# Starting layer 0 on half a tile and one weight chunk, with the rotary angles on GpSimd

## The chip, the cores and the metric

One core of one Trainium2 chip runs the whole kernel. The metric is device time in microseconds (us), the median of three runs. Engines are named as in the profile: PE is TensorE (matmuls), DVE VectorE, ACT ScalarE, POOL GpSimd, SP the engine that issues the DMAs here.

## The reference, cut to what matters

Two layers of a streaming encoder on a sequence of 256 rows and 1024 columns, in float32. Each layer is a hybrid mixer, a cross-attention and a SwiGLU block, each with a residual and a layer norm. Only the start of the first mixer is touched:

```
def rope(x, pos):
    half = x.shape[-1] // 2
    inv_freq = ROPE_BASE ** (-jnp.arange(half, dtype=jnp.float32) / half)
    ang = pos.astype(jnp.float32)[..., None] * inv_freq
    ...
    cos, sin = jnp.cos(ang), jnp.sin(ang)
...
def hybrid_mixer(x, pos, w_in, ...):
    h = x @ w_in
    a_qkv, b_cq, b_ckv, b_kr, c_qkv, c_f, g = split_cols(h, ...)
    y_a = chunked_relpos_attention(a_qkv[:, :, 0], a_qkv[:, :, 1], a_qkv[:, :, 2], a_rel_bias)
    y_b = mla_attention(b_cq, b_ckv, b_kr, pos, b_q_norm, b_kv_norm, b_w_uq, b_w_ukv)
```

The kernel begins with the 384 columns `b_cq` (PSUM tile `l0c`, one for each half of the rows), goes on with `b_ckv`, `b_kr`, `c_f` (PSUM tile `l0r`, 296 columns) and then the columns of `a_qkv` (PSUM tile `l0a`). `cos` and `sin` (tables `cc` and `ss`) rotate `b_kr` and, later, the queries of the second mixer.

## The kernel before

The rows of x are two tiles of 128 (t = 0, 1). A matmul contracts over partitions, so x is transposed on PE in eight blocks of 128 columns for each tile, four to a PSUM tile `x_t`. ACT then copies that PSUM tile to `xTh`, rounded to the matmul format, and DVE subtracts to get the rest, `xTl`. Weights come from DRAM in chunks (`raw`) and are split the same way: ACT writes `hi` (line 90), DVE writes `lo` (line 91). Each product is three matmuls, hi x hi, lo x hi and hi x lo. `raw` has three buffers, so chunk n+3 is loaded when chunk n is split.

`Chunks` keeps this stream going. `load_first` issues the first loads, `next` hands out a chunk and splits ahead. Chunks 0 and 1 are the upper and lower 512 rows of the weights for `b_cq`. Each is split in four pieces, one block of 128 rows each. Chunks 2 and 3 belong to `l0r`, chunks 4 to 7 to the four `l0a` tiles.

The order of instructions on each engine is fixed when the program is built: a scheduler walks the code, and `tc.issue_after` and priorities set what may come ahead of what. Engines then run their own lists in order and wait for each other through semaphores. Before the first real matmul PE runs `warm_up`, matmuls of the identity that nobody reads: five at the very start and six after the transposes of tile 0.

`queries(t)` does chunk 0 and then chunk 1 for tile t into `l0c`; `late=True` puts the four products with `xTl` last in each chunk. `finish(1)`, the transposes of tile 1, follows `queries(0)`. `keys(t)` makes `l0r`. The matmul results live in a pool of four PSUM banks: `l0c` and `l0r` take all four, and the four `l0a` tiles that follow need a bank that has been read out. `rotary_tables` is made once, on DVE and ACT, after the splits for the first four chunks are placed; the rows at lines 610 to 614, which read `l0r`, need its result.

Of the kernel before, what the change touches and what calls it, by code (L numbers as in the profile page):

```python
# [24 lines left out]
QL = 384  # L25
KVL = 256
NOPE = 64
ROPE = 32
# [4 lines left out]
MAGIC = 12582912.0  # L33
NEG = -1.0e30
PRIO = 400
# [13 lines left out]
class Chunks:  # L49
# [25 lines left out]
    def _split(self, i):  # L75
        kts, cols, _, slots, heads = self.plan[i]
        raw = self.raw.pop(i)
        pool, tags = (self.split_pool, ("hi", "lo")) if slots is None else (self.slot_pool, slots)
        hi = pool.tile([P, kts, cols], F32R, tag=tags[0], name=f"hi{i}")
        lo = pool.tile([P, kts, cols], F32R, tag=tags[1], name=f"lo{i}")  # L80
        n = 4 if i < 2 else 2
        for h in range(n):
            c = (slice(None), slice(None), slice(h * cols // 2, (h + 1) * cols // 2))
            if kts % 2 == 0:
                c = (slice(None), slice(h * kts // n, (h + 1) * kts // n))
            a, b, r = hi[c], lo[c], raw[c]
            if heads:
                r = r.rearrange("p k (h e d) -> p k e h d", h=heads, e=2)
                a, b = (z.rearrange("p k (e h d) -> p k e h d", h=heads, e=2) for z in (a, b))
            self.nc.scalar.copy(a, r)  # L90
            self.last_split = self.nc.vector.tensor_tensor(  # L91
                out=b, in0=r, in1=a.bitcast(F32), op=ALU.subtract
            )
        self.parts[i] = (hi, lo)
# [33 lines left out]
def encoder_kernel(  # L128
# [32 lines left out]
    W = Chunks(nc, rawp, splitp, big, 5, 1)  # L161
    for l in range(L):
# [3 lines left out]
        for c in range(2):  # L166
            r = slice(512 * c, 512 * (c + 1))
# [50 lines left out]
        xt = resid.tile([P, D], F32, tag=f"x{t}", name=f"x{t}")  # L218
        x.append(xt)

    def x_load(t):
        for h in range(2):
            c = slice(512 * h, 512 * (h + 1))
            nc.sync.dma_start(x[t][:, c], x_in[0, t * P : (t + 1) * P, c])


    x_load(0)
    W.load_first(2)
    x_load(1)
    W.load_first(4)  # L230
    ident = const.tile([P, P], F32, tag="ident", name="ident")
    make_identity(nc, ident)
# [8 lines left out]
    def load(dst, src):  # L241
        with tc.issue_after(W.last.ins):
            nc.sync.dma_start(dst, src)
# [16 lines left out]
    cc = const.tile([P, 2, ROPE], F32, tag="cc", name="cc")  # L260
    ss = const.tile([P, 2, ROPE], F32, tag="ss", name="ss")

    def rotary_tables():
        half = ROPE // 2
        pos_i = const.tile([P, 2], I32, tag="pos_i", name="pos_i")
        load(pos_i, positions)
        pos = const.tile([P, 2], F32, tag="pos", name="pos")
        nc.vector.tensor_copy(pos, pos_i)
        freq = const.tile([P, half], F32, tag="freq", name="freq")
        for i in range(half):  # L270
            nc.gpsimd.memset(freq[:, i : i + 1], 10000.0 ** (-i / half))
        halfpi = const.tile([P, 1], F32, tag="halfpi", name="halfpi")
        nc.gpsimd.memset(halfpi, math.pi / 2)
        ang = const.tile([P, 2, half], F32, tag="ang", name="ang")
        for t in range(2):
            nc.vector.tensor_scalar(
                out=ang[:, t], in0=freq, scalar1=pos[:, t : t + 1], scalar2=None, op0=ALU.mult
            )
        n = const.tile([P, 2, half], F32, tag="turn", name="turn")
        nh = const.tile([P, 2, half], F32, tag="turn_h", name="turn_h")  # L280
        nc.vector.tensor_scalar(
            out=n, in0=ang, scalar1=1.0 / (2 * math.pi), scalar2=MAGIC, op0=ALU.mult, op1=ALU.add
        )
        nc.vector.tensor_scalar(out=n, in0=n, scalar1=MAGIC, scalar2=None, op0=ALU.subtract)
        nc.vector.tensor_scalar(
            out=nh, in0=n, scalar1=1.0 / 4096, scalar2=MAGIC, op0=ALU.mult, op1=ALU.add
        )
        nc.vector.tensor_scalar(
            out=nh, in0=nh, scalar1=MAGIC, scalar2=4096.0, op0=ALU.subtract, op1=ALU.mult
        )  # L290
        nc.vector.tensor_tensor(out=n, in0=n, in1=nh, op=ALU.subtract)
        c1 = 6.28125
        c2 = round((2 * math.pi - c1) * 2**20) / 2**20
        c3 = 2 * math.pi - c1 - c2
        for c in (c1, c2, c3):
            for part in (nh, n):
                nc.vector.scalar_tensor_tensor(
                    out=ang, in0=part, scalar=-c, in1=ang, op0=ALU.mult, op1=ALU.add
                )
        lim = 3.1415925  # L300
        nc.vector.tensor_scalar(
            out=ang, in0=ang, scalar1=lim, scalar2=-lim, op0=ALU.min, op1=ALU.max
        )
        nc.scalar.activation(ss[:, :, half:], ang, AF.Sin)
        nc.vector.scalar_tensor_tensor(
            out=n, in0=ang, scalar=-1.0, in1=ang, op0=ALU.mult, op1=ALU.max
        )
        nc.scalar.activation(cc[:, :, 0:half], n, AF.Sin, bias=halfpi, scale=-1.0)
        nc.vector.tensor_copy(cc[:, :, half:], cc[:, :, 0:half])
        nc.vector.tensor_scalar(  # L310
            out=ss[:, :, 0:half], in0=ss[:, :, half:], scalar1=-1.0, scalar2=None, op0=ALU.mult
        )


    kpe = const.tile([P, 2, P], F32, tag="kpe", name="kpe")
# [13 lines left out]
            nc.vector.tensor_tensor(out=lo, in0=ps, in1=hi.bitcast(F32), op=ALU.subtract),  # L329
        )  # L330

    def transpose_in(src, hi, lo, t, name, prio=2 * PRIO):

        for g in range(2):
            ps = abank(f"{name}_t{t}{g}")
            for k in range(4):
                nc.tensor.transpose(
                    ps[:, k * P : (k + 1) * P], src[:, (4 * g + k) * P : (4 * g + k + 1) * P], ident
                )
            with tc.high_priority(prio):  # L340
                ins = split_out(
                    hi[:, 4 * g : 4 * g + 4, t * P : (t + 1) * P],
                    lo[:, 4 * g : 4 * g + 4, t * P : (t + 1) * P],
                    ps.rearrange("p (k q) -> p k q", k=4),
                )
        return ins
# [13 lines left out]
    def as_(ps, w, c, k0, act, t, kts, start=True, stop=True, at=None, late=False):  # L360

        hi, lo = w
        ah, al = act
        s = slice(t * P, (t + 1) * P)
        last = None

        def low(k):
            nonlocal last
            last = mm(ps, al[:, k0 + k, s], hi[:, k, c], start=False, stop=stop and k == kts - 1)  # L369

        for k in range(kts):
# [147 lines left out]
    def mixer(l, finish):  # L519
# [8 lines left out]

        with ExitStack() as order:
            if l == 0:  # L530
                for ins in finish(0):
                    order.enter_context(tc.issue_after(ins.ins))
                warm_up(6)
                W.ahead_split = 0
                ww = [W.next() for _ in range(2)]
                W.ahead_split = 1
            else:
                ww = [W.next() for _ in range(4)]
        pc, pr = [], []

        def queries(t):
            ps = bank(f"{name}c{t}")
            as_(ps[:, 0:QL], ww[0], slice(0, QL), 0, xT, t, 4, True, False, late=True)
            pc.append(ps)
            return as_(ps[:, 0:QL], ww[1], slice(0, QL), 4, xT, t, 4, False, True, late=True)

        def keys(t):
# [6 lines left out]
        if l == 0:  # L554
            with tc.issue_after(queries(0).ins):
                second = finish(1)
            with ExitStack() as order:
                for ins in second:
                    order.enter_context(tc.issue_after(ins.ins))
                ww += [W.next() for _ in range(2)]  # L560
            queries(1)
            keys(0)
            keys(1)
        else:
            for t in range(2):
                queries(t)
                keys(t)
                if t == 0:
                    finish(1)

        if l == 0:
            with tc.issue_after(W.last_split.ins):
                rotary_tables()

        rel = bigtile(1, name + "rel")
        nc.gpsimd.memset(rel[0:64, :, 0:64], NEG)
# [16 lines left out]
        for t in range(2):  # L593
# [7 lines left out]
            for i, ps, a, n in parts:  # L601
# [12 lines left out]
            nc.vector.tensor_tensor(  # L614
                out=z[:, t], in0=pr[t][:, KVL + ROPE : KVL + ROPE + H], in1=bf, op=ALU.add
            )

        nc.vector.scalar_tensor_tensor(out=e, in0=z, scalar=-1.0, in1=z, op0=ALU.mult, op1=ALU.min)
        nc.scalar.activation(e, e, AF.Exp)
# [501 lines left out]
        gb = load_gains(4, ln_ffn_g[l], ln_ffn_b[l], name)  # L1121
        return out_proj(FT // 2, act, 2, gb, name, last=l == L - 1, tail=3, inside=True)

    finish = lambda t: transpose_in(x[t], xTh, xTl, t, "x0", 0)
    for l in range(L):
        finish = mixer(l, finish)
        finish = cross(l, finish)
# [33 lines left out]
```

## Time and profile before

| | us |
|---|---|
| median of three runs | 1026.73 |
| lowest, highest | 1026.42, 1027.92 |
| the profiled execution, its own time | 1027.47 |
| span of that execution in the profile | 1025.8 |
| PE busy in the span | 1013.6 |
| DVE, ACT, POOL busy | 686.3, 512.5, 117.0 |

The own time of the profiled execution holds 1.67 us that lie outside the span, and it is 0.74 us above the median. A time read in the trace counts from the start of the span.

### The profile page before, as it was taken

To read this page: it belongs to the slowest core of one execution; us is meant where nothing else is said; L and a number is where in the kernel's file an instruction comes from. 1 tells how busy PE (TensorE), PEld (TensorE's weight loads), DVE (VectorE), ACT (ScalarE), POOL (GpSimd) and SP (SyncE) were. 2 spreads that over 40 slices of the span, in tenths; PEclk is the share of its full clock that TensorE was granted. 3 is DMA by queue.
4 is the path that set the end of the run, shared out by engine and by line. 5 is a ranking of instruction groups with operands and counts; after the bars stand their busy time and mean duration, and the time that the engine had idled before them with its cause. 6 is when DMAs were issued, how large, how long until landed. Compare 5 with 4: busy or idle time off the path is not lost.

```text
span 1025.8 us, 18091 instructions
## 1 busy us (share of the span) xinstructions
PE 1013.6 (99%) x7494; PEld 954.0 (93%) x7494; DVE 686.3 (67%) x1164; ACT 512.5 (50%) x842; POOL 117.0 (11%) x156
## 2 busy tenths in 40 slices
PE   9999999999999999999999999999999999999997
PEld 8988999999998999998899889999989899999996
DVE  4879777757778555554776877767659785555445
ACT  5767555555455444443355775455444634444430
POOL 3100112512001000000021002052210010000001
PEclk9999999999999999999999999999999999999999
DMA  8755645466563656565556473534775454555631
GB/s 285 210 173 158 202 143 182 136 233 213 197 214 127 202 166 203 167 243 187 185 178 193 129 241 124 163 126 127 286 244 188 149 185 157 188 187 183 236 134 42
DMA packets 133651, 186.76 MB, mean 182 GB/s; under 512 B 6064, under 2 KB 108480, under 8 KB 132800
## 3 DMA queue, kind: packets, MB, share of 16 engines
q1 hardware_dynamic: 133568, 185.60, 54.7%
q8 instruction: 59, 0.97, 0.4%
q14 instruction: 24, 0.20, 0.1%
HBM read 182.42 MB, written 3.16 MB: 181 GB/s over the span
## 4 chain that ended last, share of the span: by engine, by line
PE 94%; DVE 2%; DMA 1%; POOL 1%; issue 0%; ACT 0%; SPq 0%; POOLq 0%; DVEq 0%
PE l0g L354 2%; PE l1g L354 2%; PE l1g L356 2%; PE l0g L356 2%; PE l1g L355 2%; PE l0g L355 2%; PE f1o L373 2%; PE f1o L372 2%; PE f1o L369 2%; PE f0o L373 2%; PE f0o L372 2%; PE f0o L369 2%; PE f0u L355 2%; PE f1u L354 2%; PE f0g L355 2%; PE f1g L355 2%
## 5 line engine op out<-in xcount | busy, mean ns | idle before, releaser
L91 DVE TENSOR_TENSOR lo<-raw,hi 128x1024 fp32r<-128x1024 f32 (+3 forms) x332 | 393.2, 1203 | 196.5 <-ACT hi L90 195.9
L90 ACT CAST hi<-raw 128x1024 fp32r<-128x1024 f32 (+3 forms) x332 | 330.1, 1017 | 312.4 <-issue 156.9
L354 PE MATMUL l0g<-xTh,hi 128*128 128x256 f32 x192 | 54.2, 282 | 0.0
L354 PE MATMUL l1g<-xTh,hi 128*128 128x256 f32 x192 | 54.2, 282 | 0.0
L356 PE MATMUL l1g<-xTh,lo 128*128 128x256 f32 x192 | 53.9, 281 | 0.0
L356 PE MATMUL l0g<-xTh,lo 128*128 128x256 f32 x192 | 53.9, 281 | 0.0
L355 PE MATMUL l1g<-xTl,hi 128*128 128x256 f32 x192 | 53.9, 281 | 0.0
L355 PE MATMUL l0g<-xTl,hi 128*128 128x256 f32 x192 | 53.9, 281 | 0.0
L385 POOL TENSOR_SCALAR f_r<-f_mv 128x1 f32<-128x1 f32 x4 | 3.3, 826 | 355.1 <-DVE f_mv L415 355.1
L373 PE MATMUL f1o<-lo,f1hh 128*128 128x256 f32 (+1 forms) x132 | 42.2, 320 | 0.0
L372 PE MATMUL f1o<-hi,f1hh 128*128 128x256 f32 (+1 forms) x132 | 42.1, 319 | 0.0
L369 PE MATMUL f1o<-hi,f1hl 128*128 128x256 f32 (+1 forms) x132 | 42.0, 318 | 0.0
L354 PE MATMUL f1g<-xTh,hi 128*128 128x256 f32 x144 | 40.5, 282 | 0.0
L354 PE MATMUL f0g<-xTh,hi 128*128 128x256 f32 x144 | 40.5, 282 | 0.0
L355 PE MATMUL f1g<-xTl,hi 128*128 128x256 f32 x144 | 40.5, 281 | 0.0
L355 PE MATMUL f0g<-xTl,hi 128*128 128x256 f32 x144 | 40.5, 281 | 0.0
L356 PE MATMUL f0g<-xTh,lo 128*128 128x256 f32 x144 | 40.5, 281 | 0.0
L356 PE MATMUL f1g<-xTh,lo 128*128 128x256 f32 x144 | 40.5, 281 | 0.0
L355 PE MATMUL f0u<-xTl,hi 128*128 128x256 f32 x144 | 40.5, 281 | 0.0
L356 PE MATMUL f0u<-xTh,lo 128*128 128x256 f32 x144 | 40.5, 281 | 0.0
L354 PE MATMUL f1u<-xTh,hi 128*128 128x256 f32 x144 | 40.5, 281 | 0.0
L354 PE MATMUL f0u<-xTh,hi 128*128 128x256 f32 x144 | 40.5, 281 | 0.0
(649 smaller groups left out, 3309.3 us busy)
## 6 DMA issues: line engine op xcount, KB each, us to landing
raw<-in_w_in SPq DMA_DIRECT2D x48, 1024.0 KB, 5.3
raw<-in_ffn_w_gu SPq DMA_DIRECT2D x44, 1024.0 KB, 5.1
raw<-in_ffn_w_down SPq DMA_DIRECT2D x22, 1024.0 KB, 4.8
raw<-in_w_branch SPq DMA_DIRECT2D x12, 1024.0 KB, 5.0
raw<-in_w_mix_out SPq DMA_DIRECT2D x8, 1024.0 KB, 4.8
raw<-in_xa_w_kv SPq DMA_DIRECT2D x8, 1024.0 KB, 5.0
raw<-in_xa_w_q SPq DMA_DIRECT2D x4, 1024.0 KB, 5.0
raw<-in_xa_w_o SPq DMA_DIRECT2D x4, 1024.0 KB, 4.9
```

What stands on the lines that cost most here:

```text
L90: self.nc.scalar.copy(a, r)
L91: self.last_split = self.nc.vector.tensor_tensor(out=b, in0=r, in1=a.bitcast(F32), op=ALU.subtract)
L354: mm(ps, hi[:, k, c], ah[:, k0 + k, :], start=start and k == 0, stop=False)
L355: mm(ps, hi[:, k, c], al[:, k0 + k, :], start=False, stop=False)
L356: mm(ps, lo[:, k, c], ah[:, k0 + k, :], start=False, stop=stop and k == kts - 1)
L369: last = mm(ps, al[:, k0 + k, s], hi[:, k, c], start=False, stop=stop and k == kts - 1)
L372: mm(ps, ah[:, k0 + k, s], hi[:, k, c], start=start and k == 0, stop=False)
L373: mm(ps, ah[:, k0 + k, s], lo[:, k, c], start=False, stop=False)
L385: nc.gpsimd.tensor_scalar(out=dst, in0=src, scalar1=scale, scalar2=eps, op0=ALU.mult, op1=ALU.add)
```

## The change

Five things are done to the first microseconds of layer 0.

- The second half of x's first tile is loaded after weight chunk 0 instead of before it, and `positions` is loaded second instead of after the chunks.
- Only the first half of tile 0 is transposed and only chunk 0 is split before the matmuls begin. The other half and chunk 1 come after the matmuls of chunk 0.
- The angles for the rotary tables are computed on GpSimd. The fused multiply-add of VectorE (`scalar_tensor_tensor`) becomes two GpSimd instructions, six times over.
- The absolute value stays on VectorE, the two sines on ScalarE; they are placed after the splits of chunks 0 to 3. The copy and the sign change that fill the tables go to GpSimd.
- What follows up to the exponential of the forget gate is placed after those splits too (`order`).

```diff
-    def x_load(t):
-        for h in range(2):
-            c = slice(512 * h, 512 * (h + 1))
-            nc.sync.dma_start(x[t][:, c], x_in[0, t * P : (t + 1) * P, c])
-    x_load(0)
+    def x_load(t, h):
+        c = slice(512 * h, 512 * (h + 1))
+        nc.sync.dma_start(x[t][:, c], x_in[0, t * P : (t + 1) * P, c])
+    pos_i = const.tile([P, 2], I32, tag="pos_i", name="pos_i")
+    x_load(0, 0)
+    nc.sync.dma_start(pos_i, positions)
+    W.load_first(1)
+    x_load(0, 1)
     W.load_first(2)
-    x_load(1)
+    x_load(1, 0)
+    x_load(1, 1)
     W.load_first(4)
...
-            nc.vector.tensor_scalar(
+            nc.gpsimd.tensor_scalar(
                 out=ang[:, t], in0=freq, scalar1=pos[:, t : t + 1], scalar2=None, op0=ALU.mult
             )
...
         for c in (c1, c2, c3):
             for part in (nh, n):
-                nc.vector.scalar_tensor_tensor(
-                    out=ang, in0=part, scalar=-c, in1=ang, op0=ALU.mult, op1=ALU.add
-                )
+                nc.gpsimd.tensor_scalar(out=pc, in0=part, scalar1=-c, scalar2=None, op0=ALU.mult)
+                nc.gpsimd.tensor_tensor(out=ang, in0=ang, in1=pc, op=ALU.add)
...
+    def rotary_tables():
+        ang, n, halfpi = angles
         nc.vector.scalar_tensor_tensor(
             out=n, in0=ang, scalar=-1.0, in1=ang, op0=ALU.mult, op1=ALU.max
         )
+        nc.scalar.activation(ss[:, :, half:], ang, AF.Sin)
         nc.scalar.activation(cc[:, :, 0:half], n, AF.Sin, bias=halfpi, scale=-1.0)
-        nc.vector.tensor_copy(cc[:, :, half:], cc[:, :, 0:half])
-        nc.vector.tensor_scalar(
+        nc.gpsimd.tensor_copy(cc[:, :, half:], cc[:, :, 0:half])
+        nc.gpsimd.tensor_scalar(
             out=ss[:, :, 0:half], in0=ss[:, :, half:], scalar1=-1.0, scalar2=None, op0=ALU.mult
         )
+    angles = rotary_angles()
...
             if l == 0:
-                for ins in finish(0):
+                for ins in finish(0, (0,)):
                     order.enter_context(tc.issue_after(ins.ins))
                 warm_up(6)
                 W.ahead_split = 0
-                ww = [W.next() for _ in range(2)]
-                W.ahead_split = 1
+                ww = [W.next()]
...
         def queries(t):
             ps = bank(f"{name}c{t}")
-            as_(ps[:, 0:QL], ww[0], slice(0, QL), 0, xT, t, 4, True, False, late=True)
+            mid = as_(ps[:, 0:QL], ww[0], slice(0, QL), 0, xT, t, 4, True, False, late=True)
             pc.append(ps)
+            if len(ww) == 1:
+                with ExitStack() as order:
+                    order.enter_context(tc.issue_after(mid.ins))
+                    for ins in finish(0, (1,)):
+                        order.enter_context(tc.issue_after(ins.ins))
+                    ww.append(W.next())
             return as_(ps[:, 0:QL], ww[1], slice(0, QL), 4, xT, t, 4, False, True, late=True)
...
+        order = ExitStack()
         if l == 0:
-            with tc.issue_after(W.last_split.ins):
-                rotary_tables()
+            for ins in (W.last_split, W.last_copy):
+                order.enter_context(tc.issue_after(ins.ins))
+            rotary_tables()
```

This is PE's list before, from its first instruction to the start of chunk 1 (`hi_171`, `lo_172` are chunk 0, `hi_183`, `lo_184` chunk 1; the pairs for the other three blocks of chunk 0 are left out):

```order
L237 MATMUL warm<-ident 128x128 x5
L337 MATMUL x_t_147<-ident,x_93 128x128 x4
L337 MATMUL x_t_154<-ident,x_93 128x128 x4
L237 MATMUL warm<-ident 128x128 x6
L372 MATMUL l0c_193<-hi_171,xTh 128x384
...
L369 MATMUL l0c_193<-hi_171,xTl 128x384 x4
L372 MATMUL l0c_193<-hi_183,xTh 128x384
```

The same place in the change (`hi_211`, `lo_212` are chunk 0, `hi_243` chunk 1):

```order
L241 MATMUL warm<-ident 128x128 x5
L346 MATMUL x_t_194<-ident,x_93 128x128 x4
L241 MATMUL warm<-ident 128x128 x6
L381 MATMUL l0c_221<-hi_211,xTh 128x384
...
L378 MATMUL l0c_221<-hi_211,xTl 128x384 x4
L346 MATMUL x_t_234<-ident,x_93 128x128 x4
L381 MATMUL l0c_221<-hi_243,xTh 128x384
```

The second group of four transposes has moved from ahead of the warm-up to between the two chunks. ACT's list at the start, before:

```order
L328 CAST xTh<-x_t_147 128x4x128
L328 CAST xTh<-x_t_154 128x4x128
L90 CAST hi_171<-raw_97 128x384 x4
L90 CAST hi_183<-raw_100 128x384 x4
L599 ACTIVATE l0cn,l0sq_386<-l0c_193 128x384
L328 CAST xTh<-x_t_218 128x4x128
```

And in the change, up to the halves of chunk 4 (`hi_428`):

```order
L337 CAST xTh<-x_t_194 128x4x128
L90 CAST hi_211<-raw_98 128x384 x4
L337 CAST xTh<-x_t_234 128x4x128
L90 CAST hi_243<-raw_102 128x384 x4
L337 CAST xTh<-x_t_265 128x4x128
...
L314 ACT_TABLE_LOAD
L314 ACTIVATE ss<-ang 128x2x16
L616 ACTIVATE l0cn,l0sq_387<-l0c_221 128x384
L90 CAST hi_428<-raw_207 128x1024
L315 ACTIVATE cc<-turn,halfpi 128x2x16
L616 ACTIVATE l0cn,l0sq_403<-l0c_295 128x384
```

Chunk 1's four copies now stand behind the copy of the second half of tile 0, and the two sines stand around the first half of chunk 4. DVE's list has the same order for `xTl` and `lo`. Its later part before, where the results of the first two `l0a` tiles are read out into `l0qa`:

```order
L268 CAST pos<-pos_i 128x2
L693 SCALAR_TENSOR_TENSOR l0qa<-l0a_433,l0qa 64x2x256
L276 TENSOR_SCALAR ang<-freq,pos 128x16 x2
L91 TENSOR_TENSOR lo_550<-raw_232,hi_549 128x1024
L281 TENSOR_SCALAR turn<-ang 128x32
...
L301 TENSOR_SCALAR ang<-ang 128x32
L693 SCALAR_TENSOR_TENSOR l0qa<-l0a_494,l0qa 64x2x256
...
L610 TENSOR_TENSOR kpe<-l0r_279,cc 128x32
```

And in the change:

```order
L627 TENSOR_TENSOR kpe<-l0r_345,cc 128x32
...
L636 SCALAR_TENSOR_TENSOR l0e<-l0z 128x16
L91 TENSOR_TENSOR lo_496<-raw_241,hi_495 128x1024
L91 TENSOR_TENSOR lo_557<-raw_279,hi_556 128x1024
L639 SCALAR_TENSOR_TENSOR l0logf<-l0z,l0e 128x16
L711 SCALAR_TENSOR_TENSOR l0qa<-l0a_440,l0qa 64x2x256
```

The angle rows are gone from this stretch, and the rows that read `l0r` out of its banks stand ahead of `l0qa` instead of behind it.

## Rows read from the trace of the kernel before

**Rows 1.** The page: busy time of each engine.

```profile
PE 1013.6 (99%) x7494; PEld 954.0 (93%) x7494; DVE 686.3 (67%) x1164; ACT 512.5 (50%) x842; POOL 117.0 (11%) x156
```

**Rows 2.** One stretch: A:B length, busy PE PEld DVE ACT POOL, PEclk, DMA, GB/s.

```profile
24.54:49.11 24.57, 23.20 (x194) 22.85 (x193) 19.99 (x48) 18.56 (x25) 3.93 (x6) 1.00 0.74 222
```

**Rows 3.** Timeline of the first 14 us, PE: start, length, instruction, count.

```profile
1.77 2.50 PE L237 MATMUL warm<-ident 128*128 128x128 f32 x10 [1.77 <-POOL ident masks.py:199]
4.06 1.92 PE L337 MATMUL x_t<-ident,x 128*128 128x128 f32 x8
5.77 2.42 PE L237 MATMUL warm<-ident 128*128 128x128 f32 x12
7.95 0.42 PE L372 MATMUL l0c<-hi,xTh 128*128 128x384 f32 x1
9.53 0.86 PE L369 MATMUL l0c<-hi,xTl 128*128 128x384 f32 x4
12.31 1.04 PE L337 MATMUL x_t<-ident,x 128*128 128x128 f32 x8
13.62 0.44 PE L372 MATMUL l0c<-hi,xTh 128*128 128x384 f32 x1 [0.27 <-ACT xTh L328]
```

**Rows 4.** The same timeline, ACT, DVE and SP.

```profile
6.50 3.89 ACT L90 CAST hi<-raw 128x384 fp32r<-128x384 f32 x8
6.63 0.69 DVE L329 TENSOR_TENSOR xTl<-x_t,xTh 128x512 fp32r<-128x512 f32 x1 [0.16 <-ACT xTh L328]
7.24 3.83 DVE L91 TENSOR_TENSOR lo<-raw,hi 128x384 fp32r<-128x384 f32 x8
12.03 0.38 SPq L71 DMA_DIRECT2D raw<-in_w_in  x1
12.99 1.07 ACT L328 CAST xTh<-x_t 128x512 fp32r<-128x512 f32 x2
13.94 2.47 ACT L90 CAST hi<-raw 128x592 fp32r<-128x592 f32 x4
21.73 2.00 ACT L90 CAST hi<-raw 128x1024 fp32r<-128x1024 f32 x2 [2.98 <-DMA raw<-in_w_in]
```

**Rows 5.** Pieces of chunk 0's and 1's splits, 7.1 to 7.6 us.

```profile
7.24 0.55 DVE L91 TENSOR_TENSOR lo<-raw,hi 128x384 fp32r<-128x384 f32 x1
7.37 0.93 ACT L90 CAST hi<-raw 128x384 fp32r<-128x384 f32 x2
```

**Rows 6.** PE's timeline around the starts of the third and fourth `l0a`.

```profile
35.78 0.28 PE L356 MATMUL l0a<-xTh,lo 128*128 128x256 f32 x1
37.03 0.36 PE L354 MATMUL l0a<-xTh,hi 128*128 128x256 f32 x1 [0.97 <-DVE l0qa L693]
42.55 0.28 PE L355 MATMUL l0a<-xTl,hi 128*128 128x256 f32 x1
42.67 0.28 PE L356 MATMUL l0a<-xTh,lo 128*128 128x256 f32 x1
43.35 0.36 PE L354 MATMUL l0a<-xTh,hi 128*128 128x256 f32 x1 [0.40 <-DVE l0qa L693]
```

**Rows 7.** POOL's timeline: scaling of a column, a table, and an add.

```profile
13.18 0.19 POOL L385 TENSOR_SCALAR l0rs<-l0sq 128x1 f32<-128x1 f32 x1 [7.51 <-ACT l0cn L599]
13.46 0.56 POOL L388 TENSOR_TENSOR l0rs<-l0rs,nhalf 128x1 f32<-128x1 f32 x1
24.18 1.04 POOL L385 TENSOR_SCALAR l0rs<-l0sq 128x1 f32<-128x1 f32 x1 [4.52 <-ACT l0cn L599]
39.89 0.39 POOL L588 TENSOR_SCALAR l0hb<-l0hb 128x24 f32<-128x24 f32 x1 [10.84 <-DMA l0hb<-in_b_gate]
```

**Rows 8.** DVE and POOL timelines at 250 us: two splits and an add.

```profile
248.12 1.22 DVE L91 TENSOR_TENSOR lo<-raw,hi 128x1024 fp32r<-128x1024 f32 x1 [0.45 <-ACT hi L90]
249.85 3.45 DVE L91 TENSOR_TENSOR lo<-raw,hi 128x1024 fp32r<-128x1024 f32 x2
250.11 2.12 POOL L855 TENSOR_TENSOR l0acc<-l0acc,l0th 128x512 f32<-128x512 f32 x1 [7.26 <-DVE l0th L851]
```

More of the change, by code (lines that the diff above doesn't have):

```diff
@@ L89, in _split @@
                 a, b = (z.rearrange("p k (e h d) -> p k e h d", h=heads, e=2) for z in (a, b))
-            self.nc.scalar.copy(a, r)
+            self.last_copy = self.nc.scalar.copy(a, r)
             self.last_split = self.nc.vector.tensor_tensor(
@@ L261, in encoder_kernel, with rotary_angles @@
     ss = const.tile([P, 2, ROPE], F32, tag="ss", name="ss")
[L263 to L266, printed above, removed]
+    half = ROPE // 2
+    def rotary_angles():
         pos = const.tile([P, 2], F32, tag="pos", name="pos")
-        nc.vector.tensor_copy(pos, pos_i)
+        nc.gpsimd.tensor_copy(pos, pos_i)
         freq = const.tile([P, half], F32, tag="freq", name="freq")
@@ L280, in rotary_tables @@
         nh = const.tile([P, 2, half], F32, tag="turn_h", name="turn_h")
-        nc.vector.tensor_scalar(
+        nc.gpsimd.tensor_scalar(
             out=n, in0=ang, scalar1=1.0 / (2 * math.pi), scalar2=MAGIC, op0=ALU.mult, op1=ALU.add
         )
-        nc.vector.tensor_scalar(out=n, in0=n, scalar1=MAGIC, scalar2=None, op0=ALU.subtract)
-        nc.vector.tensor_scalar(
+        nc.gpsimd.tensor_scalar(out=n, in0=n, scalar1=MAGIC, scalar2=None, op0=ALU.subtract)
+        nc.gpsimd.tensor_scalar(
             out=nh, in0=n, scalar1=1.0 / 4096, scalar2=MAGIC, op0=ALU.mult, op1=ALU.add
         )
-        nc.vector.tensor_scalar(
+        nc.gpsimd.tensor_scalar(
             out=nh, in0=nh, scalar1=MAGIC, scalar2=4096.0, op0=ALU.subtract, op1=ALU.mult
         )
-        nc.vector.tensor_tensor(out=n, in0=n, in1=nh, op=ALU.subtract)
+        nc.gpsimd.tensor_tensor(out=n, in0=n, in1=nh, op=ALU.subtract)
+        pc = const.tile([P, 2, half], F32, tag="turn_c", name="turn_c")
         c1 = 6.28125
@@ L296, in rotary_tables @@
             for part in (nh, n):
-                nc.vector.scalar_tensor_tensor(
-                    out=ang, in0=part, scalar=-c, in1=ang, op0=ALU.mult, op1=ALU.add
-                )
+                nc.gpsimd.tensor_scalar(out=pc, in0=part, scalar1=-c, scalar2=None, op0=ALU.mult)
+                nc.gpsimd.tensor_tensor(out=ang, in0=ang, in1=pc, op=ALU.add)
         lim = 3.1415925
-        nc.vector.tensor_scalar(
+        nc.gpsimd.tensor_scalar(
             out=ang, in0=ang, scalar1=lim, scalar2=-lim, op0=ALU.min, op1=ALU.max
         )
-        nc.scalar.activation(ss[:, :, half:], ang, AF.Sin)
+        return ang, n, halfpi
+    def rotary_tables():
+        ang, n, halfpi = angles
         nc.vector.scalar_tensor_tensor(
@@ L307, in rotary_tables @@
         )
+        nc.scalar.activation(ss[:, :, half:], ang, AF.Sin)
         nc.scalar.activation(cc[:, :, 0:half], n, AF.Sin, bias=halfpi, scale=-1.0)
-        nc.vector.tensor_copy(cc[:, :, half:], cc[:, :, 0:half])
-        nc.vector.tensor_scalar(
+        nc.gpsimd.tensor_copy(cc[:, :, half:], cc[:, :, 0:half])
+        nc.gpsimd.tensor_scalar(
             out=ss[:, :, 0:half], in0=ss[:, :, half:], scalar1=-1.0, scalar2=None, op0=ALU.mult
         )
+    angles = rotary_angles()
     kpe = const.tile([P, 2, P], F32, tag="kpe", name="kpe")
@@ L330, in split_out, with transpose_in @@
         )
-    def transpose_in(src, hi, lo, t, name, prio=2 * PRIO):
-        for g in range(2):
+    def transpose_in(src, hi, lo, t, name, prio=2 * PRIO, halves=(0, 1)):
+        for g in halves:
             ps = abank(f"{name}_t{t}{g}")
@@ L560, in mixer @@
                 ww += [W.next() for _ in range(2)]
+            W.ahead_split = 1
             queries(1)
@@ L616, in mixer @@
             )
+        order.close()
         nc.vector.scalar_tensor_tensor(out=e, in0=z, scalar=-1.0, in1=z, op0=ALU.mult, op1=ALU.min)
@@ L1122, in ffn @@
         return out_proj(FT // 2, act, 2, gb, name, last=l == L - 1, tail=3, inside=True)
-    finish = lambda t: transpose_in(x[t], xTh, xTl, t, "x0", 0)
+    finish = lambda t, halves=(0, 1): transpose_in(x[t], xTh, xTl, t, "x0", 0, halves)
     for l in range(L):
```

## The prediction

> **What bounds the kernel now.** I began with the page: PE is busy for 99% of the span [rows 1], so only a change that takes waits away from PE, or takes work off it, can shorten the kernel. The change leaves PE's matmuls as they are and touches the first 50 us. The reader should therefore look for PE's waits there. Rows of POOL, DVE and ACT count only where PE waits for them.
>
> I then read the timeline of PE up to 14 us [rows 3]. The ten records of the first warm-up run from 1.77 us, the transposes from 4.06, twelve more warm-up records from 5.77, and the first matmul that counts starts at 7.95. The reader should see that nothing useful is done between 5.77 and 7.95. Chunk 0's four last products start at 9.53, the transposes of tile 1 at 12.31, and its first matmul at 13.62 after a wait for ACT's copy.
>
> The speed of PE changes in this stretch. Eight transposes from 4.06 to 5.77 are 0.214 us apart; the same eight from 12.31 have their last end after 1.04 us, some 0.11 apart [rows 3]. The granted clock stands at 1.00 in the rows of this trace [rows 2], but the pace of the same instruction tells the two levels apart: 1.2 GHz first, 2.4 GHz later. Twelve warm-up records in 2.18 us (5.77 to 7.95) are eight at 0.214 and four at 0.11, so the clock rose near 7.5 us, with PE busy since 1.77.
>
> Third, I read the stretch with the four `l0a` tiles: in 24.57 us PE is busy for 23.20 [rows 2]. The timeline shows where [rows 6]. Matmuls start 0.12 apart (42.55, 42.67). The third `l0a` starts 1.25 us after the matmul before it, the fourth 0.68 after. That is 1.13 + 0.56 = 1.69 us lost, and the releaser is both times DVE's `l0qa`, which empties the bank of an earlier `l0a`.
>
> **The change part by part.**
>
> *The matmuls of chunk 0 start earlier.* Four transposes fewer stand ahead of the warm-up: at 0.214 each, 0.85 us. The warm-up then begins at 4.92. If the clock still rises near 7.5, its twelve records last 2.57 us instead of 2.18 and end near 7.48, so the first matmul comes 0.47 us earlier. It then goes at 0.17 us a matmul unless data is late: the four that start at 9.53 last 0.86 together [rows 3], three paces and the last one's length, which is about two paces (0.28 against 0.12 in [rows 6]). Before, the last of the chunk's twelve matmuls started at 9.53 + 3 x 0.17 = 10.05, because one `lo` piece was late; now, at 7.48 + 11 x 0.17 = 9.35. The pieces allow it: ACT's first copy of chunk 0 follows one `xTh` instead of two, 0.85 us earlier than 6.50 [rows 4]. The `lo` pieces, 0.47 apart (3.83 us for eight, 0.55 the last [rows 4, 5]), end at about 8.35, and the fourth is wanted at 8.67. The weights bound it: ACT took the third piece only at 7.37, when it had landed [rows 5]. If the loads are no faster than before, the last `lo` ends at 8.92 and the last matmul starts at 9.66. If the warm-up took 2.18 as before, the `lo` pieces would set the last start to 9.09. So this term is -0.39 to -0.96 us; I take -0.70. The load of `positions` costs SP one issue slot, the one that the second half of x gives up, so chunk 0 is issued when it was. The second half of x is not wanted before 9.5.
>
> *A hole opens between the chunks.* This is the cost. Call the start of chunk 0's last matmul L. Before, chunk 1 was already being split by then and the transposes of tile 1 came 2.26 us after L (12.31 against 10.05). Now the chain is serial, since on PE, ACT and DVE chunk 1 stands behind the second half of tile 0:
>
> - PE's transposes start at L + 0.18. ACT's copy started 0.68 after the first transpose (12.31 to 12.99), so `xTh` at L + 0.86.
> - ACT's next copy follows after 0.49 (two take 1.07, one of them 0.59 [rows 4]), so the first `hi` piece of chunk 1 starts at L + 1.35.
> - DVE's `xTl` follows the start of `xTh` by 0.62 (12.99 to 13.61, by the same step as at 6.63), at L + 1.48. The first `lo` comes 0.61 behind it (6.63 to 7.24 [rows 4]), at L + 2.09, and the fourth 3 x 0.467 later, at L + 3.49. It ends at L + 4.04.
> - PE's product with it starts at about L + 4.10, four more follow 0.17 apart, and tile 1's transposes start at L + 4.96.
>
> The price is 4.96 - 2.26 = 2.70 us. From tile 1's transposes on, the order is the old one up to `l0r`, so PE carries 2.70 - 0.70 = +2.00 us into the first `l0a`, at 26.5 instead of 24.5.
>
> *The wait in `l0a` goes.* Seventeen of DVE's eighteen rotary instructions leave its list, and the rows that empty `l0r` come ahead of `l0qa`. The third and fourth `l0a` then have banks that DVE has emptied before. I take the whole 1.69 us as gained. The bounds are 1.69 and 0, if another result is late in its place.
>
> *What GpSimd takes on.* There are 21 instructions up to the angles. Scaling a column took 0.19, 24 columns 0.39, with 0.09 from one to the next (13.18, 0.19, 13.46) [rows 7]. So 20 instructions on 32 columns are 5.6 to 9.6 us, and the fills that stand among them are those POOL did before. Starting at about 4 to 6 us they end at 13 to 19. The sine waits for them behind the last copy of chunk 3, which ended at 16.41 and moves to 18.4 [rows 4]. So they are hidden, if only just at the upper end.
>
> *The sines and the table load.* ACT waited 2.98 us for chunk 4's load, which came at 21.73 [rows 4]. The load of the sine's table and the first sine fit in there. Behind them are queued the squares of `l0c` and, on POOL, the scalings for which DVE's `l0cn` waits, with the `lo` pieces of chunk 4 behind that. Chunk 4 is loaded when chunk 1's raw buffer is free, at L + 4.04 = 13.4 instead of 12.03. With the same 9.7 us to land it is there at 23.1, which is late for its second half by at most 0.6 us; with less traffic ahead of it, not at all. I take 0, and keep 0.6 for the range.
>
> *GpSimd beside VectorE's splits.* POOL's scaling took 1.04 us beside a split against 0.19 alone [rows 7], so here POOL waits and the split does not. But at 249.85 two splits took 3.45 us, where one is 1.22, and the add of 512 columns stands beside them [rows 8]: there the split waited about 1.1 us. So the short angle instructions can cost each of chunk 1's four `lo` pieces from nothing to one instruction of 0.39, 0 to 1.56 us together. I take 0.2, nearer the row with a short instruction.
> The Trainium skill, "SBUF — State Buffer", section "Who interferes with whom", says that a VectorE instruction with two inputs in SBUF and a GpSimd instruction that reads SBUF exclude each other, and that whichever comes second waits it out. The trace agrees that both sides can wait. By that rule alone, with GpSimd always first, this term would be its upper end.
>
> *The sum.* -0.70 + 2.70 - 1.69 + 0.20 = +0.5 us. The profiled execution's span would go from 1025.8 to 1026.3, its own time from 1027.47 to 1028.0; that one is 0.74 above the median, so the median goes from 1026.73 to 1027.2. A difference within 0.2% (2.05 us) can't be told from no change here.
>
> **The rivals.**
>
> *Slower: PE's clock falls in the hole.* From L + 0.6 to L + 1.95 PE has nothing, and up to L + 4.1 it waits for pieces, so that from 9.4 to 14.3 it works for about half the time. At the start it ran at the lower level from 1.77 to 7.5, 5.7 us. If it fell back for as long, it would do half as much in it, 2.9 us lost: 1030.1. It decides from 1.6 us lost. Against it: in the 1.3 us between 12.31 and 13.62, with a wait in it, it did not fall.
>
> *GpSimd's locks take their full price.* The first sum becomes +1.9: 1028.6, just inside 0.2%.
>
> *The wait stays.* If `l0a` finds another late result, the 1.69 us are not won, and with up to 0.6 for chunk 4 the sum is +2.2 to +2.8: 1029.2, slower. For it: the chain sines, squares, scalings, `l0cn`, `lo` is long. Against it: the third `l0a` starts 11 us behind the first.
>
> *Faster.* If the hole were covered, only -0.70 - 1.69 are left: 1024.3. It needs the second half of tile 0 to be copied while chunk 0's matmuls run; the order stands against it.
>
> **How the numbers follow.** I give the sum 64%, the full locks 12%, the fall of the clock 11%, the wait that stays 8%, the covered hole 5%. Slower by over 0.2%: 11 + 5 of the 8 + 2 of the 12, about 18%; faster 5%; the same 77%. The predicted time is 1027.2. The sum's own bounds are -0.96 + 2.70 - 1.69 = +0.05 and -0.39 + 2.70 - 1.69 + 1.56 + 0.60 = +2.78, so 1026.8 to 1029.5. The range goes 1 us further down, half way to the covered hole with the runs' own spread, and holds most of the wait that stays: 1025.8 to 1029.4.
>
> **What would show it.** The first `l0c` near 7.5 us; a hole of over 1 us on PE after the second four transposes; tile 1's transposes near 14.3; no wait for `l0qa` in `l0a`; and the transposes after the fourth `l0a` at 49 to 50 us, where they were at 49.1. I am wrong if the hole is missing, if matmuls behind it are 0.32 apart instead of 0.17, or if chunk 4 is awaited.

## The result and the profile after

The changed kernel takes 1034.34 us (median of 4 runs, 1034.03 to 1035.52) against 1026.86 for the kernel before (4 runs beside them, 1026.42 to 1027.92): a ratio of 1.0068, 95% interval 1.0056 to 1.008. It is slower by 7.5 us, outside the range of 1025.8 to 1029.4. Of all the runs told of below, one execution of `rot_only_x32` took 1653.68 us at a mean granted clock of 0.557, and no ratio counts it.

The page has PE as busy as before by share, and 7.9 us longer, with the same count of instructions [rows 1]:

```profile
span 1033.7 us, 18097 instructions
...
PE 1021.5 (99%) x7494; PEld 961.6 (93%) x7494; DVE 683.2 (66%) x1147; ACT 511.1 (49%) x842; POOL 123.8 (12%) x179
```

PE's waits up to 60 us (us in total, times, longest) show no `l0qa` any more; the hole between the chunks is there, 1.1 us for the first `hi` piece:

```profile
PE warm L241 <- POOL ident masks.py:199: 1.8, 1, 1.8
PE l0c L381 <- ACT hi L90: 1.1, 1, 1.1
PE l0c L382 <- DVE lo L91: 0.4, 1, 0.4
PE l0c L381 <- ACT xTh L337: 0.2, 1, 0.2
```

PE's timeline of the start, to be held against [rows 3]:

```profile
4.06 1.06 PE L346 MATMUL x_t<-ident,x 128*128 128x128 f32 x4
4.92 2.00 PE L241 MATMUL warm<-ident 128*128 128x128 f32 x12
6.67 0.42 PE L381 MATMUL l0c<-hi,xTh 128*128 128x384 f32 x1
...
8.69 0.88 PE L378 MATMUL l0c<-hi,xTl 128*128 128x384 f32 x4
9.40 0.60 PE L346 MATMUL x_t<-ident,x 128*128 128x128 f32 x4
11.09 0.45 PE L381 MATMUL l0c<-hi,xTh 128*128 128x384 f32 x1 [1.09 <-ACT hi L90]
...
13.39 0.52 PE L381 MATMUL l0c<-hi,xTh 128*128 128x384 f32 x1
13.71 0.52 PE L382 MATMUL l0c<-lo,xTh 128*128 128x384 f32 x1
14.04 1.48 PE L378 MATMUL l0c<-hi,xTl 128*128 128x384 f32 x4
15.31 1.47 PE L346 MATMUL x_t<-ident,x 128*128 128x128 f32 x8
17.02 0.46 PE L381 MATMUL l0c<-hi,xTh 128*128 128x384 f32 x1 [0.24 <-ACT xTh L337]
```

Matmuls start 0.32 apart at 13.39, and the four products with `xTl` last 0.88 us ahead of the hole and 1.48 behind it: PE runs at the lower level there, the sign that the prediction named. The same stretch by windows (length, busy PE PEld DVE ACT POOL, granted clock, DMA, GB/s):

```profile
4.92:12.70 7.78, 6.33 (x34) 4.91 (x33) 4.62 (x9) 4.47 (x10) 6.66 (x17) 1.00 1.05 352
12.70:16.10 3.40, 3.40 (x13) 3.10 (x12) 0.63 (x2) 0.00 (x0) 1.96 (x7) 0.51 0.84 182
```

From 12.7 to 16.1 the granted clock is 0.51 of full speed, 1.2 GHz. That is the prediction's rival "PE's clock falls in the hole". It explains little of the loss, though. The transposes behind the fourth `l0a` start 1.8 us later than before, before's row first:

```profile
L630 PE MATMUL l0cT<-ident,l0cn x10: 272/272/273, 49.1 to 50.1; 128*128 128x128 f32 x10
```

```profile
L648 PE MATMUL l0cT<-ident,l0cn x10: 272/272/273, 50.9 to 51.9; 128*128 128x128 f32 x10
```

So over 6 of the 7.9 us come later, where the change was not looked for. First start on PE of some tiles, from `l0r` to the last output `f1o` (us, from the trace), and how much later:

| tile | l0r | l0a | l0cT | l0g | l0mixo | f0g | f0o | l1g | f1g | f1o |
|---|---|---|---|---|---|---|---|---|---|---|
| before | 18.0 | 24.5 | 49.1 | 93.5 | 248.1 | 350.8 | 453.5 | 597.8 | 853.3 | 956.0 |
| after | 21.3 | 27.9 | 50.9 | 95.0 | 250.7 | 354.1 | 458.2 | 602.4 | 859.8 | 963.9 |
| later by | 3.3 | 3.4 | 1.8 | 1.5 | 2.6 | 3.3 | 4.7 | 4.6 | 6.5 | 7.9 |

The delay grows where `ws`, a helper of the kernel, multiplies weights with 256 columns of `xTh` or `xTl` (from `l0g` on, from `f0g` to `f0o`, from `f1g` to `f1o`) and stands still between `f0o` and `l1g`. PE has no wait in the feed-forward stretch: 80 us in the middle of the first block, before and then after (PE alone; behind the x is the count of matmuls, then the granted clock, the DMA share and GB/s).

```profile
360.00:440.00 80.00, 80.00 (x679) 1.00 0.56 185
```

```profile
360.00:440.00 80.00, 80.00 (x669) 1.00 0.55 182
```

In the same 80 us, at the same full clock, PE gets through 669 matmuls instead of 679. Without the two or three that were running at the window's start, that is 0.120 us a matmul instead of 0.118. The kernel has some 3800 matmuls of this kind on `xTh` and `xTl`.

### The profile page after: what moved, and what is told of

Same layout as the page of the kernel before. It is cut to its first block, busy times and chain, and to the rows that moved or that the text cites. A ratio compares the mean times of both kernels' runs of the same rounds, so it can differ in the third digit from the quotient of the medians.

```text
span 1033.7 us, 18097 instructions
## 1 busy us (share of the span) xinstructions
PE 1021.5 (99%) x7494; PEld 961.6 (93%) x7494; DVE 683.2 (66%) x1147; ACT 511.1 (49%) x842; POOL 123.8 (12%) x179
## 3 DMA queue, kind: packets, MB, share of 16 engines
HBM read 182.42 MB, written 3.16 MB: 180 GB/s over the span
## 4 chain that ended last, share of the span: by engine, by line
PE 97%; DVE 1%; POOL 0%; issue 0%; ACT 0%; POOLq 0%; DVEq 0%
PE l0g L363 2%; PE l1g L363 2%; PE l1g L365 2%; PE l0g L365 2%; PE l1g L364 2%; PE l0g L364 2%; PE f1o L382 2%; PE f1o L381 2%; PE f1o L378 2%; PE f0o L382 2%; PE f0o L378 2%; PE f0o L381 2%; PE f1u L365 2%; PE f1u L364 2%; PE f1u L363 2%; PE f0u L365 2%
## 5 line engine op out<-in xcount | busy, mean ns | idle before, releaser
L364 PE MATMUL f1u<-xTl,hi 128*128 128x256 f32 x144 | 40.8, 283 | 0.0
L365 PE MATMUL f1u<-xTh,lo 128*128 128x256 f32 x144 | 40.8, 283 | 0.0
```

Of the source, the lines that this page charges most:

```text
L364: mm(ps, hi[:, k, c], al[:, k0 + k, :], start=False, stop=False)
L365: mm(ps, lo[:, k, c], ah[:, k0 + k, :], start=False, stop=stop and k == kts - 1)
```

## The experiments

What differs for those matmuls is where their operands lie. A matmul has two of them: the weights, which PEld loads, and the moving operand, here `xTh` or `xTl`. "Distance" below is the address of the moving operand minus that of the weights, modulo 256 bytes. The new tile `turn_c` and the earlier place of the rotary tiles move `xTh` and `xTl` by 672 bytes in a partition and everything behind them by 128. Theory A: the addresses set the pace. Rivals: B, the array came out of the second rise of the clock in another step; C, the order of the instructions. Ratios below go against runs of the kernel before on the same chip (medians 1027.96 to 1028.59 there). The addresses in the built programs (bytes in a partition; `w` is the split weights, the big tiles hold results between the stages; the last two columns are modulo 256, which at first I did not know to matter):

```
kernel           xTh     w        xTh - w   big tiles - w
before           13984   178880   224       0
after            14656   179008   0         0
after_x32        14688   179072   224       0
before_x0        14016   178944   192       0
after_w32        14656   179040   224       224
after_x32_w32    14688   179104   192       224
after_b0         14656   179072   192       0
before_x0_b64    14016   179072   64        192
after_w64        14656   179072   192       192
```

### Moving xTh and xTl by 32 bytes: after_x32, before_x0

```diff
+    const.tile([P, 8], F32, tag="pad0", name="pad0")
     xTh = const.tile([P, KT, T], F32R, tag="xTh", name="xTh")
     xTl = const.tile([P, KT, T], F32R, tag="xTl", name="xTl")
+    const.tile([P, 8], F32, tag="pad1", name="pad1")
```

Expected of after_x32:

> The changed kernel with 32 unused bytes ahead of xTh and 32 behind xTl: both start again 32 bytes past a multiple of 64, as in the kernel before, and nothing else changes. Theory A, the address: the 256-column matmuls that read xTh or xTl run at 118.3 ns instead of 120.0, so 3840 of them give back 6.1 us, 384 with xT as weights 0.9, and some 190 of 512 columns cost 1.2 more: 1034.3 - 5.8 = 1028.5 us. Theory B, the clock that fell and rose a second time left the array in a slower step: 1034.3, pace 120.0. Theory C, the changed order of the instructions: 1034.3 too.

Measured: 1028.48 us (10 runs), ratio 1.0002, interval 0.9993 to 1.0012. The 7.5 us are gone with 32 bytes; the order is that of after, so C falls. The window from 360 to 440 us has the count of before:

```profile
360.00:440.00 80.00, 80.00 (x678) 1.00 0.57 185
```

The granted clock was 1.00 from 12.7 to 16.1 in this execution, so B is left to the next runs. The first starts are 20.1 (`l0r`), 26.7 (`l0a`), 49.4 (`l0cT`), 351.2 (`f0g`), 956.4 (`f1o`): 0.3 us later than before at `l0cT`, and 0.4 at the end. The drift is gone.

Expected of before_x0:

> The kernel before with the same 2 x 32 unused bytes, which puts xTh and xTl on multiples of 64, as in the changed kernel. Theory A: 1026.9 + 5.8 = 1032.7 us with the old start, pace 120.0 in the gate and feed-forward stages. Theories B and C: 1026.9, pace 118.3 as before.

Measured: 1009.8 us (4 runs), ratio 0.982, interval 0.9803 to 0.9836. My rule of "32 bytes past a multiple of 64" was wrong in the other direction: here the two lie on multiples of 64, and the kernel before gains 18 us. Its window has 708 matmuls, 0.113 us each:

```profile
360.00:440.00 80.00, 80.00 (x708) 1.00 0.59 191
```

### Moving the weights too: after_w32, after_x32_w32

```diff
+    pool("padp", 1).tile([P, 8], F32, tag="pad2", name="pad2")
     splitp = pool("splitp", 3)
```

> The changed kernel, xTh and xTl on multiples of 64, but the split weights of all chunks (hi, lo) 32 bytes past one. If what counts is that the two operands of a matmul lie differently within 64 bytes, the gate and feed-forward matmuls run at 118.3, those on ya, yb, yc and on mem too (another 1.2 us), and the 512-column ones go from 227 to 234 (about 6 us lost): 1031 to 1033. If only the moving operand counts, the weight-stationary ones stay at 120.0 and only the 512-column ones change: 1034 to 1040. If only xT's own address counts: 1034.3 and no pace changes.

Measured: 1032.07 (one run), 678 matmuls in the window. Moving the weights by 32 does what moving xT did, so it is the distance that counts. The 512-column matmuls went from 0.227 to 0.233, about as expected, and the clock fell in the hole in this execution, as in after (last value but two in the second line):

```profile
360.00:440.00 80.00, 80.00 (x678) 1.00 0.57 183
12.70:16.10 3.40, 3.40 (x14) 0.53 0.88 212
```

With the fall, but at the other distance, the pace is 0.118: B falls.

> The changed kernel with xTh, xTl and the split weights all 32 bytes past a multiple of 64. If it is the difference between the two operands that counts, the matmuls on xT are back at 120.0 and those on ya, yb, yc and mem at 118.3: 1034 to 1039, by what the 512-column ones with weights from big tiles lose. If an offset by itself makes a matmul faster: xT's at 118.3 or below, 1026 to 1029.

Measured: 1023.09 (one run), 681 matmuls in the window, but a quicker `l0a`. Both moved by 32, the time is neither that of after (1034.3) nor that of after_x32. Neither expectation held: the paddings add up, xTh moved by 32 and the weights by 96, so the distance is a third one, 192, the same as in before_x0. Modulo 64 the two runs and after would all lie at 0, with three different times; so the next runs take the distance modulo more than 64.

### The pace by itself: bench

This kernel leaves the whole encoder out and copies x to the output. It runs 96 matmuls a stretch:

```
w[:, dw // 4 + 128 * (i % 8) : ...]   x[:, dx // 4 + cols * (i % 4) : ...]
za 0,0  zb 0,32  zc 0,64  zd 0,96  ze 0,128  zf 0,160  zg 0,192  zh 0,224  zi 0,256  zj 0,16   (dw, dx in bytes)
zk 32,32  zl 64,64  zm 64,0  zn 32,0      256 columns; zo 0,0  zp 0,32  zq 0,64  zr 64,0   512 columns
```

> No encoder at all: 20 stretches of 96 matmuls each on one set of weights and one moving operand in SBUF, with nothing else running; only the offsets of the two operands differ (the output is a copy of x). Theory A1, the difference of the two addresses modulo 128 bytes sets the pace of 256-column matmuls: 120 ns at a difference of 0 (za, ze, zi, zk, zl), 118 at 32 and 96 (zb, zd, zf, zh, zn), 113 to 114 at 64 (zc, zg, zm). Theory A2, the address of one operand alone: zk and zl differ from za. Theory A3, it needs the other engines' traffic: all stretches alike. 512 columns: 227 at 0, 234 at 32, 226 to 232 at 64.

PE's timeline of it (start, length, instruction, count):

```profile
20.89 11.68 PE L76 MATMUL za<-x,w 128*128 128x256 f32 x96
32.41 11.47 PE L76 MATMUL zb<-x,w 128*128 128x256 f32 x96
43.73 11.47 PE L76 MATMUL zc<-x,w 128*128 128x256 f32 x96
55.04 11.67 PE L76 MATMUL zd<-x,w 128*128 128x256 f32 x96
66.54 11.56 PE L76 MATMUL ze<-x,w 128*128 128x256 f32 x96
...
89.20 11.07 PE L76 MATMUL zg<-x,w 128*128 128x256 f32 x96
100.11 11.52 PE L76 MATMUL zh<-x,w 128*128 128x256 f32 x96
111.47 11.68 PE L76 MATMUL zi<-x,w 128*128 128x256 f32 x96
122.98 11.56 PE L76 MATMUL zj<-x,w 128*128 128x256 f32 x96
...
145.89 11.67 PE L76 MATMUL zl<-x,w 128*128 128x256 f32 x96
157.40 11.07 PE L76 MATMUL zm<-x,w 128*128 128x256 f32 x96
168.30 11.52 PE L76 MATMUL zn<-x,w 128*128 128x256 f32 x96
179.66 21.95 PE L76 MATMUL zo<-x,w 128*128 128x512 f32 x96
201.45 22.57 PE L76 MATMUL zp<-x,w 128*128 128x512 f32 x96
```

The pace of a stretch is the time from its start to the next one's, over 96. By distance: 0 bytes 120.0 ns (za; zl the same, 119.9), 32 117.9, 64 117.8, 96 119.8, 128 118.6, 192 113.6, 224 118.3, and 256 again 119.9. zm (weights 64, moving 0) is distance 192 once more, 113.5, and zn is 224, 118.3. So in these stretches the pace goes with the difference of the two addresses modulo 256, with no other engine at work: A2 (one address alone) and A3 (other engines' traffic) fall, and A1's modulo of 128 was too short. For 512 columns the order is another: 227.0 at 0 (zo), 233.3 at 32 (zp).

The windows of five runs fit it: before, after_x32 and after_w32 lie at 224 (118.3), after at 0 (120.0), before_x0 at 192 (113.6). after_x32_w32 fits it in part: at 192 its `l0a` went at 113.4 ns, but its window at 117.8.

### The changed kernel at distance 192: after_b0, after_b0_fill, and a distance that misses

after_b0 has 64 unused bytes behind x's tiles (`resid.tile([P, 16], F32, ...)`); after_b0_fill adds warm-up matmuls in the hole:

```diff
                     ww.append(W.next())
+                warm_up(6)
...
             mm(ps, ah[:, k0 + k, s], hi[:, k, c], start=start and k == 0, stop=False)
+            if fill:
+                warm_up(1)
```

> The changed kernel with 64 unused bytes behind x's tiles, which moves every later tile by 64: the split weights now lie 64 away from xTh and xTl within 128 bytes, as in the run of the kernel before with xT moved. Theory A1: the matmuls on xT at 113 to 114 ns, so 1009.8 us and what the new start costs, 0.3 without a fall of the clock, 1.5 with one: 1010 to 1011.5. If the pace came from something else that the old program has: 1028 to 1034.

Measured: 1014.14 (4 runs, 1012.26 to 1019.03), ratio 0.987, interval 0.9843 to 0.9898. The gain came, but not all. The two feed-forward blocks, one window each, say why: the first ran at 708, the second at 682, each through the whole block.

```profile
360.00:440.00 80.00, 80.00 (x708) 1.00 0.58 190
862.00:942.00 80.00, 80.00 (x682) 1.00 0.57 186
```

At this distance a feed-forward block holds either of two paces, 0.113 or 0.118, which is 3.8 us a block here. The same program differs from run to run by 7 us; that this comes from the two paces is likely but not shown, since one execution of it was profiled.

> The same, with 6 warm-up multiplications behind the transposes of the second half and one more behind each first matmul of chunk 1's k tiles, so that TensorE has work in the hole. If the fall of the clock in the hole is what costs 1.2 us in the executions that have it: no fall in the profile, and 0 to 1.2 us under the run without them. If the warm-ups get in the way of chunk 1's matmuls: 0.3 to 1 us over it.

Measured: 1015.18 (4 runs, 1011.98 to 1016.31), which can't be told from the run without the warm-ups. `l0cT` started at 50.0 against 48.7, so they got in the way by 1.3 us; the clock fell in neither execution. On what a fall costs it says nothing.

before_x0_b64 has the pads of before_x0, 64 bytes behind x's tiles and 64 ahead of the weights:

> The kernel before with xTh, xTl and all big tiles at 64 and the split weights at 0 modulo 128 bytes. Theory A1: the 576 matmuls on ya, yb, yc and the 192 on mem go from 120 to 114 ns too (4.6 us), the last 264 of the feed-forward output gain up to 1, and some 780 of 512 columns lose 2 ns each (1.6 us): 1009.8 - 4 = 1006 us. If only xT counts: 1009.8.

Measured: 1022.72 (10 runs, 1017.08 to 1027.45), ratio 0.9942, interval 0.9919 to 0.9964. I had reckoned modulo 128; modulo 256 the distance for xT is 64, where bench gives 117.8, and the window has 681. The expectation was wrong, and for the window the rule of bench right. The spread of 10 us between its runs is not explained.

### Each half of the change alone: rot_only_x32, half_only

half_only is the kernel before with the new start (loads, half tile, one chunk); rot_only_x32 is the changed kernel with the old start, and with `positions` loaded behind chunk 1:

```diff
-                for ins in finish(0, (0,)):
+                for ins in finish(0):
...
-                ww = [W.next()]
+                ww = [W.next() for _ in range(2)]
+                W.ahead_split = 1
```

Both have xT at distance 224, like the kernel before.

> The old start (x's first tile whole, both weight chunks split at once), only the angles on GpSimd and the sines behind the splits; xTh and xTl 32 bytes on, so that they stand to the weights as in the kernel before. If the two halves of the change add up as predicted, the wait for l0qa is gone (-1.69) and the start costs nothing: l0cT 1.5 to 1.7 us earlier, 1025.3 us. If the wait only moves to chunk 4 or to the sines: 1026.9.

Measured: 1028.82 (11 runs), ratio 1.0008, interval 1.0 to 1.0017. The wait for `l0qa` is gone, and PE waits longer for something else; ACT's timeline shows for what:

```profile
PE l0a L364 <- DVE l0cn L620: 2.3, 1, 2.3
```

```profile
21.39 2.00 ACT L90 CAST hi<-raw 128x1024 fp32r<-128x1024 f32 x2 [4.91 <-DMA raw<-in_w_in]
23.41 1.28 ACT L313 ACT_TABLE_LOAD   x1
24.71 0.23 ACT L313 ACTIVATE ss<-ang 128x32 f32<-128x32 f32 x1
24.84 0.47 ACT L617 ACTIVATE l0cn<-l0c 128x384 f32<-128x384 f32 x1
```

Chunk 4's split, which waits 4.91 us for its load, stands ahead of the sine's table load, and the squares that lead to `l0cn` and so free `l0a`'s first bank stand behind it.

> The new start (half a tile, one chunk at a time), with the rotary angles on VectorE as before; every tile at its old address. If the hole costs +2.70 and the earlier start gives 0.70: l0r 2.0 us later, and the wait for l0qa, which is counted from the splits, stays: 1028.9. If PE's delay swallows that wait: 1027.2. A fall of the clock in the hole: 1.2 more.

Measured: 1029.03 (11 runs), ratio 1.0011, interval 1.0002 to 1.0019. `l0r` starts at 20.0, 2.0 us later, as the terms said. The wait for `l0qa` shrinks but stays:

```profile
PE l0a L356 <- DVE l0qa L701: 0.7, 1, 0.7
```

`l0cT` starts at 50.3, +1.2. So at `l0cT` the new start alone costs 1.2 us, rot_only_x32 costs 0.8 (49.9), and the whole change 0.3. But rot_only_x32 is not simply the other half: in it ACT splits chunk 4 ahead of the sines, an order that the changed kernel does not have.

### One line in the changed kernel: after_w64, and rot_only_w64

```diff
+    pool("padp", 1).tile([P, 16], F32, tag="pad2", name="pad2")
     splitp = pool("splitp", 3)
```

> The changed kernel with those 64 bytes ahead of the split weights and nothing else. As the run above, plus the 1.7 to 2.0 us that the new start costs against the old one with the angles on GpSimd (3.2 with a fall of the clock): 1006 to 1014 us; without any effect of the distance 1034.3.

Measured: 1015.78 (4 runs, 1015.44 to 1018.2), ratio 0.9886, interval 0.9872 to 0.9899. Above the range: the profile has 682 and 681 in the two windows, both blocks in the slower step.

> The old start with the angles on GpSimd, and 64 unused bytes ahead of the split weights: xTh, xTl and the big tiles then lie 192 bytes ahead of the weights modulo 256, the distance at which the stretches measured alone ran at 113.6 ns. Theory A2, the distance modulo 256: matmuls on xT, ya to yc and mem at 113.5 to 117.8 (a stage can hold either): 1004 to 1011 us. If only xT's gain comes: 1008 to 1013.

Measured: 1018.89 (6 runs, 1009.18 to 1021.59), ratio 0.9886, interval 0.9851 to 0.9921. The same gain, with the largest spread, and above both expected ranges. In the profiled execution (1021.0) both windows have 682, and the clock fell at 27.4 us, behind a wait of 2.4 us for `l0cn`.

### The old start with the angles on GpSimd, put right: rot2_x32, rot2_b0

As rot_only, but `positions` is loaded behind the first half of x and `W.ahead_split = 1` stays where the changed kernel has it, so that the sines come ahead of chunk 4's split. The start is the old one, so this is the angles' half of the change alone.

> The old start with the angles on GpSimd once more, now with the positions loaded right behind the first half of x's tile and the sines ahead of chunk 4's split, as in the changed kernel; xTh and xTl 32 bytes on. If the wait of 2.3 us in the run before it came from the sines' table load standing behind chunk 4's late split: no wait ahead of l0a, the wait for l0qa gone too, l0cT 1.5 to 1.9 us earlier than in the kernel before, and the whole 0.15 to 0.2% faster than it. If l0a's first bank comes free late whenever layer 0's keys start at 18.0: the wait stays, and the time is that of the kernel before or 1 us over it.

Measured: 1026.18 (9 runs), ratio 0.9979, interval 0.997 to 0.9989. The table load now ends ahead of chunk 4's load:

```profile
17.33 1.28 ACT L313 ACT_TABLE_LOAD   x1
...
22.01 2.00 ACT L90 CAST hi<-raw 128x1024 fp32r<-128x1024 f32 x2 [2.00 <-DMA raw<-in_w_in]
```

PE waits for nothing in `l0a`. From `l0r` (18.9, +0.9) to `l0cT` (48.2, -0.9) PE gains 1.8 us. The +0.9 is a late chunk 0 in this execution, for whose load ACT waited 0.71 us where it had no wait before [rows 4]; rot2_b0 has the same start and `l0r` at 18.1:

```profile
7.53 4.03 ACT L90 CAST hi<-raw 128x384 fp32r<-128x384 f32 x8 [0.71 <-DMA raw<-in_w_in]
```

This is the part of the change that pays.

> The same start with xTh and xTl 192 bytes ahead of the weights modulo 256 and the big tiles in step with the weights, the distances of the kernel before with xT moved (1009.8). With the wait gone as well: 1008; with one feed-forward stage in the slower of its two steps 1012, with both 1016.

Measured: 1008.34 (5 runs, 1008.14 to 1009.21), ratio 0.9804, interval 0.979 to 0.9819: the fastest of all, 708 in the window. It is 1.8 to 2.1% under the kernel before; 0.2% of that is the angles' half of the change (rot2_x32), the rest the distance.

## Why the prediction was wrong

**The step that failed** is in its first paragraph: "The change leaves PE's matmuls as they are and touches the first 50 us." The matmuls are the same, their operands lie elsewhere. The prediction had no term for it, neither in the sum nor among the rivals, and so looked at 50 of 1026 us. By ratio the step is worth 1.0068 - 1.0002, 0.66% or 6.8 us (after against after_x32).

**The terms of the sum held.** By the execution of after_x32:

- *Earlier start and hole*, -0.70 + 2.70 = +2.00 at `l0r`: measured +2.1 (20.1 against 18.0), and +2.0 in half_only. Each part held: chunk 0's last product started at 9.36 (predicted 9.35), tile 1's transposes 5.10 behind it (4.96). Between executions `l0r` varies: 17.9 to 19.0 with the old start in seven profiles, 19.9 to 20.4 with the new one in the five without a fall or a fill. The first `l0c` was predicted at 7.48; it came at 6.67 in the profiled execution of after, whose clock rose earlier (twelve warm-up records in 2.00 us, before 2.42 [rows 3]).
- *The wait in `l0a` goes*, -1.69: between `l0r` and `l0cT` PE gained 2.1 - 0.3 = 1.8.
- *GpSimd and the sines*, +0.20 and 0: PE waits for neither in after. Beside the angles VectorE's four `lo` pieces of chunk 1 took 2.04 us, against 1.95 by the prediction's own steps (3 x 0.467 + 0.55), so some 0.1. The 0 hangs on ACT's order: with the sines behind chunk 4's split (rot_only_x32) it is 2.3.
- *The sum*, +0.5: +0.3 at `l0cT` from one execution each, and the ratio of 1.0002 with an interval on both sides of 1.

**The rival "PE's clock falls in the hole"** (11%, +2.9 us) came true in the profiled execution of after and in that of after_w32, not in five others with this hole and no fill. It cost 1.2 us there, `l0r` 3.3 later instead of 2.1, less than the 2.9 I gave it: the stretch at the lower level lasted 3.4 us, not 5.7, and without a fall PE waits for pieces for part of that stretch (busy 3.16 of 3.40 us in after_x32). The other three timed executions of after have a granted clock of 0.998 to 0.999 instead of 0.997 and spans 1.0 to 1.4 us shorter. So the fall is in the profile and, it seems, hardly in the median.

**Not settled**: what makes a stage take the one or the other pace at distance 192, and why the distance matters at all. In the profiles the feed-forward blocks at 192 ran at the quicker pace in 6 of 8 where the big tiles lie at 0 to the weights (before_x0, after_b0, after_b0_fill, rot2_b0), and in none of 6 where they do not (after_x32_w32, after_w64, rot_only_w64). No run tests this, and one timed execution of rot_only_w64 took 1009.18 us, so it may be chance. A clash of the two read streams in the memory would be a guess; no run tests that either.

## What to carry to other kernels

A new tile of 128 bytes can cost more than the edit that needs it: where a kernel lives from thousands of alike matmuls, compare the distance of their two operands modulo 256 before and after, and put it where a short bench of it is fastest. When a whole stage drifts with no wait in it, count its instructions in a fixed window of both traces before looking for a cause at the place of the edit. Half of a change, run alone, can bring an order of instructions that the whole does not have: rot_only_x32 lost 0.8 us by `l0cT`, and the same half with the sines ahead of the split, as the whole has them, gained 0.9. So compare the engines' lists before reading a half as a term.

## What the runs showed of the hardware

- Back-to-back fp32r matmuls of 256 columns at the full clock started 113.5 to 120.0 ns apart by the distance of their operands alone. The Trainium skill, "SBUF — State Buffer", section "Who interferes with whom", gives TensorE two independent read ports, one for the moving operand and one for the weights, and says that it waits on nobody. With nothing else running, bench measures 120.0 ns at distance 0 and 113.5 at 192: here the pace does depend on how the two operands lie to each other. What links them is not shown.
- For 512 columns the best distance measured is another: 227.0 ns at 0, 233.3 at 32 and at 192. Two tiles that are multiplied in both widths can't have both; but in rot2_b0 `xTh` lies at 192 for the 256-column matmuls and the big tiles, which feed most of the 512-column ones, at 0.
- The clock fell behind 1.1 us without work and sparse work after it, in some executions of the same start and not in others. In rot_only_w64 it fell behind a wait of 2.4 us ahead of `l0a` (0.57 from 27 to 31 us); in rot_only_x32 a wait of 2.3 us there brought no fall. In before_x0_b64 it fell in the middle of `l0a`, after a wait of 2.7 us there (third value from the end):

```profile
40.00:44.00 4.00, 4.00 (x24) 0.60 1.00 348
```
